# Expert inputs gathered as token rows from DRAM and transposed, in place of one-hot products; twelve weight tiles fetched ahead, not eight

## Chip, cores, metric

The kernel runs on one core of one Trainium2 chip. The metric is the device time of one launch in microseconds (us). TensorE, its weight loads, VectorE, ScalarE, GpSimd and SyncE are called PE, PEld, DVE, ACT, POOL and SP below, as in the profile.

## The reference

Two transformer blocks over 512 tokens of width 1024, in float32. The part that matters here is the mixture of experts at the end of the first block: each token is routed to two of 32 experts, and each expert multiplies its own tokens with its own weights.

```python
g_probs = softmax(hf @ w_group_router + b);  g_gate, g_sel = top_k(g_probs, 1)
e_probs = softmax(e_logits of group g_sel);  e_gate, e_sel = top_k(e_probs, 2)
...
xb = h_pad[tok]                                   # the tokens of one expert
hidden = silu(xb @ w_gate[e]) * (xb @ w_up[e])    # 1024 -> 256
y = (hidden @ w_down[e]) * wt[:, None]            # 256 -> 1024
out = zeros.at[slot_token].add(y)                 # back to the tokens
```

Ahead of it stand differential and latent attention and a cross attention to a memory; behind it the second block: a gated DeltaNet layer, a feed-forward layer, sliding-window attention and another feed-forward layer.

## The kernel before

All activations are kept with the features on the partitions and the 512 tokens along the free axis: `self.x` is eight tiles of 128 by 512. A product of full precision is split in three (`mm3`, L400 to L402): both operands have a high and a low part, and high times high, high times low and low times high are added in PSUM.

The expert stage is `moe` (L1394). It begins with the router: a product with the router weights (`few`), and then a long chain of small DVE operations (L1439 to L1510) from the logits `lt` to `As` (which expert a token goes to), from there by four small products on PE (L1498, L1500) to `posm` (the place of each token among those of its expert, one column for each of the 32 experts). An expert has 64 slots; should one get more tokens, the branch `overflow` does the rest (it isn't taken with these inputs). Beside the router the tokens are turned: 64 PE transposes (L1424) bring the high and the low part of the normalised tokens to two tiles `toks`, with the tokens on the partitions.

The experts are then done in eight rounds `q` of four experts (256 slots), and in a round in two pairs `p`. `gather(q)` makes a matrix `G` of ones and zeros by comparing `posm` with the slot numbers (L1555, DVE), and multiplies `toks` with it on PE (L1565, 64 products of 128 by 256 into `pgt`; ACT copies each bank to `xg`, L1567). That picks the tokens of the slots. Eight small products `pm` (L1571) give for each slot its weight, its token's number and its scale. `gate_up` multiplies with gate and up weights (`pgu`), `down` with the down weights (`py`, both at L1549), and `scatter` (L1615, `psx`) adds the result back to the tokens with another matrix of ones and zeros, `S`.

The expert weights, 192 tiles of 512 KB, come over SP's queue in the order of use (`experts`, `fetch`, L375). `NPRE` of them are fetched during the cross attention, nine more while the keys and values of the second block's memory are made (`mem_kv2`, 192 products of 128 by 256, which stand between router and experts to fill PE), and the rest into a ring of 17 tiles (NPRE plus nine), each as soon as the tile before it there has been read. After `moe` the next stage `gdn` begins by loading its constants `cst_gdn`.

The code isn't executed as written: a scheduler orders the instructions of each engine ahead of time, and each engine then follows its list in order.

Of the kernel before, what the change touches and what calls it, by code (L numbers as in the profile page):

```python
# [19 lines left out]
NPRE=8  # L20
# [258 lines left out]
class K:  # L279
# [1114 lines left out]
    def moe(self):  # L1394
        tc, nc, d = self.tc, self.nc, self.d
        with ExitStack() as st:
            e = lambda **k: st.enter_context(tc.tile_pool(**k))
            mp = e(name="moep", bufs=1)
            I = self.cst("ident")
            self.cst_load(mp, "moe")  # L1400
            rows = mp.tile([P, 36], F32, name="rowsr")
            nc.scalar.dma_start(rows, d["rows2"][:, 24:60].to_broadcast([P, 36]))
            toks = [mp.tile([P, 4, 1024], F32R, name=f"tok{k}") for k in range(2)]
# [4 lines left out]
            gq = e(name="mg", bufs=2)  # L1408

            with ExitStack() as s2:  # L1410
# [8 lines left out]
                for k in range(2):  # L1419
                    for t in range(4):  # L1420
                        for b in range(2):
                            pt = pp.tile([P, 512], F32, name="pl", tag="pl")
                            for c in range(4):
                                nc.tensor.transpose(pt[:, c * P:(c + 1) * P],  # L1424
                                                    hs[4 * b + c][k][:, t * P:(t + 1) * P].bitcast(F32), I)
                            o = toks[k][:, t, b * 512:(b + 1) * 512]
                            if b:
                                nc.vector.tensor_copy(o, pt)
                            else:
                                nc.scalar.activation(o, pt, AF.Copy)  # L1430
# [90 lines left out]

                if self.on("gdn"):
                    self.mem_kv2()

# [8 lines left out]
            r = self.rings["raw"]  # L1533
            used = last // 2 * 2
            self.rings, self.turn = {"raw": r[used:] + [self.pre] * NPRE + r[:used]}, {"raw": 0}
            sw = e(name="ms", bufs=2)
# [13 lines left out]

            def gather(q):

                G = gq.tile([P, 4, 256], F32R, name="G", tag="G")
                for t in range(4):
                    nc.vector.tensor_tensor(G[:, t].rearrange("p (a b) -> p a b", a=4),  # L1555
                                            self.cst("iota64").unsqueeze(1).to_broadcast([P, 4, 64]),
                                            posm[:, t, 4 * q:4 * q + 4].unsqueeze(2).to_broadcast([P, 4, 64]), OP.is_equal)
                xg = xgs[q % 2]
                for c in range(0, 8, 2):
                    pgt = self.pmm.tile([P, 512], F32, name="pgt", tag="mm")  # L1560
                    for j in range(2):
                        cs = slice((c + j) * P, (c + j + 1) * P)
                        for k in range(2):
                            for t in range(4):
                                nc.tensor.matmul(pgt[:, 256 * j:256 * j + 256], toks[k][:, t, cs], G[:, t],  # L1565
                                                 start=k + t == 0, stop=k + t == 4)
                    nc.scalar.activation(xg[:, c:c + 2].rearrange("p a b -> p (a b)"), pgt, AF.Copy)  # L1567
                pm = self.pmm.tile([P, 512], F32, name="pm", tag="mm")
                for a in range(2):
                    for t in range(4):  # L1570
                        nc.tensor.matmul(pm[:, 8 * a:8 * a + 8], G[:, t, P * a:P * a + P], meta[:, t, 2 * q + a],  # L1571
                                         start=t == 0, stop=t == 3)
                ms = gq.tile([P, 2, 8], F32, name="msl", tag="msl")
                nc.vector.tensor_copy(ms, pm[:, 0:16].rearrange("p (a b) -> p a b", a=2))
                nc.vector.tensor_tensor(ms[:, :, 0:2], ms[:, :, 0:2], ms[:, :, 2:4], OP.add)
                nc.vector.tensor_tensor(ms[:, :, 0:2], ms[:, :, 0:2],
                                        self.cst("half").unsqueeze(1).to_broadcast([P, 2, 2]), OP.mult)
                nc.vector.tensor_tensor(ms[:, :, 0:1], ms[:, :, 0:1], ms[:, :, 1:2], OP.add)
                nc.vector.tensor_tensor(ms[:, :, 6:7], ms[:, :, 6:7], ms[:, :, 7:8], OP.add)
                return xg, ms  # L1580
# [37 lines left out]
            xgs = [t.rearrange("p a (b c) -> p (a b) c", b=2).bitcast(F32) for t in self.half()]  # L1618
            g = gather(0)
            sg = gate_up(0, *g)  # L1620
            for q in range(8):
# [556 lines left out]
```

## Time and profile before

| | |
|---|---|
| time, median of 3 runs | 2052.8 us (2051.84 to 2054.6) |
| profiled execution, its time / its span | 2053.69 us / 2051.9 us |
| PE busy | 1984.0 us, 97% of the span |
| DVE, ACT, POOL busy | 50%, 36%, 17% |
| data moved by DMA | 243.44 MB, 119 GB/s over the span |
| expert stage: first expert product, end of the last | 445.72 us, 751.21 us |

The span is what the profile covers; the time lies a little above it. Times in the rows are microseconds from the start of the span, unless marked ns. "Busy" counts the time in which an engine executes instructions; what stands in square brackets behind a row is how long the engine sat idle before it, and what ended that.

### The profile page before, as it was taken

Reading aid. Unit: us, or ns where it says so; the run is one execution under the profiler, and the core shown is the slowest. Engines: PE = TensorE matmul, PEld = TensorE weight load, DVE = VectorE, ACT = ScalarE, POOL = GpSimd, SP = SyncE. Lnnn points to the kernel's source line nnn. Section 1 sums busy time; section 2 is a strip of 40 time slices with the busy share of each in tenths; the row PEclk is TensorE's granted clock in tenths of the full one; section 3 lists DMA queues with packets and bytes.
Section 4 is the critical chain, followed back from the end, with each engine's and each line's share of the span. In section 5 each row is a group of like instructions: output and inputs, shape, how many; then the busy total and the mean of one; then the engine's idle time right before and its main releaser. Section 6 shows DMA issues by size and latency. Waiting matters only on the chain.

```text
span 2051.9 us, 26341 instructions
## 1 busy us (share of the span) xinstructions
PE 1984.0 (97%) x10094; PEld 1521.2 (74%) x10094; DVE 1024.5 (50%) x2067; ACT 735.6 (36%) x1445; POOL 347.7 (17%) x328
## 2 busy tenths in 40 slices
PE   8999999899999999999998999999999999999997
PEld 6768678775555558778877888888876688888886
DVE  7674746632222246788865543343436654434334
ACT  5554644521111133344453332232325642223231
POOL 3012241300000002355411110011111021101111
PEclk9988999999999999999999999999999999999999
DMA  5213114269888852211113222322221033233322
GB/s 191 62 63 108 42 52 159 70 211 391 294 306 331 322 187 64 65 42 53 52 52 102 82 86 85 117 93 81 94 92 42 11 104 102 78 106 105 99 78 70
DMA packets 75458, 243.44 MB, mean 119 GB/s; under 512 B 8825, under 2 KB 11969, under 8 KB 75329
## 3 DMA queue, kind: packets, MB, share of 16 engines
q1 hardware_dynamic: 73520, 240.34, 34.9%
q8 instruction: 81, 1.33, 0.3%
q10 hardware_dynamic: 1664, 1.34, 0.2%
q14 instruction: 49, 0.39, 0.1%
q0 software_dynamic: 144, 0.04, 0.0%
HBM read 235.36 MB, written 6.29 MB: 118 GB/s over the span
## 4 chain that ended last, share of the span: by engine, by line
PE 72%; DVE 3%; DMA 1%; ACT 1%; POOL 1%; issue 0%; DVEq 0%; ACTq 0%
PE mmp L400 16%; PE mmp L401 16%; PE mmp L402 16%; PE pgu L1549 6%; PE psx L1615 3%; PE py L1549 3%; PE pgt L1565 3%; PE sc L1328 1%; DMA raw<-in_w_swa_dram 1%; PE po L749 1%; DVE lo L408 1%; PE tp L962 1%; PE po L1354 1%; PE pt L1340 0%; DVE cv L950 0%; PE sc L729 0%
## 5 line engine op out<-in xcount | busy, mean ns | idle before, releaser
L400 PE MATMUL mmp<-xh,hi 128*128 128x512 f32 (+1 forms) x1328 | 522.2, 393 | 0.8 <-ACT xh L407 0.7
L401 PE MATMUL mmp<-xl,hi 128*128 128x512 f32 (+1 forms) x1328 | 516.9, 389 | 1.0 <-DVE xl L411 1.0
L402 PE MATMUL mmp<-xh,lo 128*128 128x512 f32 (+1 forms) x1328 | 516.7, 389 | 0.0
L407 ACT ACTIVATE hi<-raw 128x1024 fp32r<-128x1024 f32 (+2 forms) x256 | 252.4, 987 | 646.5 <-PE mmp L401 573.7
L408 DVE TENSOR_TENSOR lo<-raw,hi 128x1024 fp32r<-128x1024 f32 (+1 forms) x242 | 280.7, 1161 | 141.5 <-ACT hi L407 138.6
L400 PEld LDWEIGHTS mmp<-xh,hi 128*128 128x128 f32 x1328 | 252.6, 190 | 57.4 <-issue 5.7
L401 PEld LDWEIGHTS mmp<-xl,hi 128*128 128x128 f32 x1328 | 252.6, 190 | 49.9 <-DVE xl L411 1.4
L402 PEld LDWEIGHTS mmp<-xh,lo 128*128 128x128 f32 x1328 | 252.2, 190 | 50.0 <-issue 0.7
L808 POOL TENSOR_TENSOR g<-g,rbc 128x512 f32<-128x512 f32 x44 | 75.1, 1707 | 508.9 <-ACT g L807 508.9
L400 PE MATMUL mmp<-ahi,hi 128*128 128x512 f32 (+1 forms) x374 | 141.9, 380 | 0.0
L401 PE MATMUL mmp<-alo,hi 128*128 128x512 f32 (+1 forms) x374 | 141.9, 380 | 0.0
L402 PE MATMUL mmp<-ahi,lo 128*128 128x512 f32 (+1 forms) x374 | 141.9, 379 | 0.0
L434 POOL TENSOR_TENSOR sqt<-sqt 128x512 f32<-128x512 f32 (+1 forms) x50 | 70.4, 1408 | 252.3 <-ACT sqt L430 236.0
L810 DVE TENSOR_TENSOR a<-mmp,g 128x512 f32<-128x512 f32 x44 | 30.4, 691 | 144.8 <-PE mmp L402 144.8
L806 DVE TENSOR_TENSOR g<-mmp,rbc 128x512 f32<-128x512 f32 x44 | 30.4, 691 | 112.8 <-PE mmp L402 112.7
L400 PEld LDWEIGHTS mmp<-ahi,hi 128*128 128x128 f32 x374 | 70.4, 188 | 14.1
L401 PEld LDWEIGHTS mmp<-alo,hi 128*128 128x128 f32 x374 | 70.4, 188 | 14.0
L402 PEld LDWEIGHTS mmp<-ahi,lo 128*128 128x128 f32 x374 | 70.4, 188 | 14.0
L1565 PEld LDWEIGHTS pgt<-G,tok 128*128 128x128 f32 x512 | 61.6, 188 | 10.9 <-issue 8.9
L1616 DVE TENSOR_TENSOR x<-psx,x 128x512 f32<-128x512 f32 x64 | 43.4, 688 | 47.5 <-PE psx L1615 46.6
L1565 PE MATMUL pgt<-G,tok 128*128 128x256 f32 x512 | 64.6, 282 | 1.0 <-ACT xl L1567 1.0
L1549 PE MATMUL py<-raw,act 128*64 128x512 f32 x256 | 63.9, 599 | 0.2
(519 smaller groups left out, 3001.2 us busy)
## 6 DMA issues: line engine op xcount, KB each, us to landing
raw<-in_w_egu_dram SPq DMA_DIRECT2D x128, 512.0 KB, 7.5
raw<-in_w_gu_dram SPq DMA_DIRECT2D x88, 512.0 KB, 3.5
raw<-in_w_ed_dram SPq DMA_DIRECT2D x64, 512.0 KB, 7.8
raw<-in_w_out_dram SPq DMA_DIRECT2D x24, 512.0 KB, 3.6
raw<-in_w_gdn_dram SPq DMA_DIRECT2D x24, 512.0 KB, 3.6
raw<-in_w_dn_dram SPq DMA_DIRECT2D x32, 384.0 KB, 3.0
raw<-in_w_dn_dram SPq DMA_DIRECT2D x32, 320.0 KB, 2.8
raw<-in_w_qk_dram SPq DMA_DIRECT2D x12, 512.0 KB, 4.3
```

The lines of the kernel that those rows point to most:

```text
L400: mm(ps, a[0], b[0], start=first, stop=False)
L401: mm(ps, a[0], b[1], start=False, stop=False)
L402: mm(ps, a[1], b[0], start=False, stop=last)
L407: nc.scalar.activation(hi, src, AF.Copy)
L408: (eng or nc.vector).tensor_tensor(lo, src, hi.bitcast(F32), OP.subtract)
L434: (nc.vector if i == len(chunks) - 1 else nc.gpsimd).tensor_tensor(acc, acc, s, OP.add)
L806: nc.vector.tensor_tensor(g, pg, bc, OP.mult)
L808: nc.gpsimd.tensor_tensor(g, g, bc, OP.mult)
L1549: nc.tensor.matmul(ps[hb], a[:, hb], w[b][:, o:o + 512], start=first, stop=last)
L1565: nc.tensor.matmul(pgt[:, 256 * j:256 * j + 256], toks[k][:, t, cs], G[:, t], start=k + t == 0, stop=k + t == 4)
L1615: nc.tensor.matmul(psx, ys[k][:, a, c * P:(c + 1) * P], ss[a], start=a + k == 0, stop=a + k == 2)
L1616: nc.vector.tensor_tensor(self.x[c], psx, self.x[c], OP.add)
```

## The change

The token matrix `toks` in SBUF is gone. The tokens (now in one part, in float32: `x` times the gain of the norm, on DVE) are transposed with 32 PE transposes instead of 64 and written to a DRAM tensor `tokd`, one row of 4 KB for each token (eight DMAs, issued by ACT). `gather` is cut in two. `slots(q)` makes `G` and the eight `pm` products as before, forms from them the token number of each slot (`idx`, DVE), and lets POOL issue two indirect DMAs, each of which fetches 128 rows of `tokd` to a tile `rows`. `gather(q, rows)` transposes these rows on PE, 16 transposes in place of 64 products, and ACT copies them to `xg` as before. `slots` is called one round ahead of its `gather`. The scale of the tokens is applied where it was before. The room that `toks` took goes to four `rows` tiles and to four more weight tiles (NPRE 12): the ring has 21 tiles.

```diff
-NPRE=8
+NPRE=12
...
-            toks = [mp.tile([P, 4, 1024], F32R, name=f"tok{k}") for k in range(2)]
+            dp = e(name="tokd", bufs=1, space=bass.MemoryType.DRAM)
+            tokd = dp.tile([T, D], F32, name="tokd")
...
+            def slots(q, room=None):
+                G = gq.tile([P, 4, 256], F32R, name="G", tag="G")
+                for t in range(4):
+                    nc.vector.tensor_tensor(G[:, t].rearrange("p (a b) -> p a b", a=4),
...
+                pm = self.pmm.tile([P, 512], F32, name="pm", tag="mm")
+                for a in range(2):
+                    for t in range(4):
+                        nc.tensor.matmul(pm[:, 8 * a:8 * a + 8], G[:, t, P * a:P * a + P], meta[:, t, 2 * q + a],
+                                         start=t == 0, stop=t == 3)
+                ms = gq.tile([P, 2, 8], F32, name="msl", tag="msl", bufs=3)
+                nc.vector.tensor_copy(ms, pm[:, 0:16].rearrange("p (a b) -> p a b", a=2))
+                idx = gq.tile([P, 2], I32, name="idx", tag="idx", bufs=3)
+                nc.vector.tensor_scalar(idx, ms[:, :, 4], 1.0, 0.0, op0=OP.subtract, op1=OP.max)
+                rows = []
+                for a in range(2):
+                    r = room() if room else gr.tile([P, D], F32, name="rows", tag="rows")
+                    nc.gpsimd.indirect_dma_start(r, None, tokd, bass.IndirectOffsetOnAxis(idx[:, a:a + 1], 0))
+                    rows.append(r)
...
+                return rows, ms
+            def gather(q, rows):
+                xg = xgs[q % 2]
+                for c in range(0, 8, 2):
+                    pgt = self.pmm.tile([P, 2, 2, P], F32, name="pgt", tag="mm")
+                    for j in range(2):
+                        for a in range(2):
+                            nc.tensor.transpose(pgt[:, j, a], rows[a][:, (c + j) * P:(c + j + 1) * P], I)
+                    nc.scalar.activation(xg[:, c:c + 2], pgt.rearrange("p j a b -> p j (a b)"), AF.Copy)
+                return xg
...
-                for k in range(2):
-                    for t in range(4):
-                        for b in range(2):
-                            pt = pp.tile([P, 512], F32, name="pl", tag="pl")
-                            for c in range(4):
-                                nc.tensor.transpose(pt[:, c * P:(c + 1) * P],
-                                                    hs[4 * b + c][k][:, t * P:(t + 1) * P].bitcast(F32), I)
-                            o = toks[k][:, t, b * 512:(b + 1) * 512]
...
+                for b in range(2):
...
+                        nc.vector.tensor_scalar(t, self.x[4 * b + c], self.sm("norm_ffn_g", 4 * b + c, 4 * b + c + 1), None,
+                                                op0=OP.mult)
...
+                            nc.tensor.transpose(pt[:, c * P:(c + 1) * P], xg[c][:, t * P:(t + 1) * P], I)
...
+                        nc.scalar.dma_start(tokd[t * P:(t + 1) * P, b * 512:b * 512 + 512], o)
...
+                sl = slots(0, lambda: r1.tile([P, D], F32, name="rows", tag="xg", bufs=3))
                 if self.on("gdn"):
                     self.mem_kv2()
+                g = gather(0, sl[0]), sl[1]
...
+            gr = e(name="mr", bufs=4)
...
-                for c in range(0, 8, 2):
-                    pgt = self.pmm.tile([P, 512], F32, name="pgt", tag="mm")
-                    for j in range(2):
-                        cs = slice((c + j) * P, (c + j + 1) * P)
-                        for k in range(2):
-                            for t in range(4):
-                                nc.tensor.matmul(pgt[:, 256 * j:256 * j + 256], toks[k][:, t, cs], G[:, t],
-                                                 start=k + t == 0, stop=k + t == 4)
...
-            g = gather(0)
+            sl = slots(1)
...
-                        g = gather(q + 1)
+                        g = gather(q + 1, sl[0]), sl[1]
+                        if q < 6:
+                            sl = slots(q + 2)
```

What the scheduler makes of it is seen at three places. The first is PE between router and experts. Before, the four products that need the router's `As` (L1498, L1500) stand among the products of `mem_kv2` (L400 to L402), 72 of which are ahead of them:

```order
L400 MATMUL mmp_4032<-hi_4028,xh_3899 128x256
L401 MATMUL mmp_4032<-lo_4029,xh_3899 128x256
L402 MATMUL mmp_4032<-hi_4028,xl_3900 128x256
L1498 MATMUL pl_3866<-As_3857,cst_moe_3590 128x128
L1500 MATMUL pl_3866<-As_3857,ones_87 128x96
L1500 MATMUL pl_3866<-As_3857,ones_87 128x64
L1500 MATMUL pl_3866<-As_3857,ones_87 128x32
L400 MATMUL mmp_4058<-hi_4024,xh_3899 128x256
L401 MATMUL mmp_4058<-lo_4025,xh_3899 128x256
L402 MATMUL mmp_4058<-hi_4024,xl_3900 128x256
```

With the change the same four (now L1546, L1548), the transpose for the overflow flag (L1556) and the `pm` products of round 0 (L1421) stand right behind the router's statistics (`stp`, `stb`), and all 192 products of `mem_kv2` follow:

```order
L549 MATMUL mmp<-cst_all,fewo 128x64 x4
L438 MATMUL stp<-ones,sqt 128x1 x4
L451 MATMUL stb<-cst_all,rt 128x128 x4
L1546 MATMUL pl<-As,cst_moe 128x128
L1548 MATMUL pl<-As,ones 128x96
L1548 MATMUL pl<-As,ones 128x64
L1548 MATMUL pl<-As,ones 128x32
L1556 MATMUL pl<-cst_all,mx 1x128
L1421 MATMUL pm<-meta,G 128x8
L438 MATMUL stp<-ones,sqt 128x1 x2
L1421 MATMUL pm<-meta,G 128x8 x7
L451 MATMUL stb<-cst_all,rt 128x128 x2
```

So what the router's DVE chain feeds has moved ahead of the products that stood around it.

The second place is PE in a round of the expert loop. Before, a quarter of `gather` is 16 products (two halves of a bank, each from `tok0` and `tok1`), here the one ahead of four products with down weights:

```order
L1615 MATMUL psx_4913<-S_4673,xh_4669 128x512
L1615 MATMUL psx_4913<-S_4673,xl_4670 128x512
L1565 MATMUL pgt_4990<-G_4985,tok0_3594 128x256 x4
L1565 MATMUL pgt_4990<-G_4985,tok1_3595 128x256 x4
L1565 MATMUL pgt_4990<-G_4985,tok0_3594 128x256 x4
L1565 MATMUL pgt_4990<-G_4985,tok1_3595 128x256 x4
L1549 MATMUL py_5118<-raw_5127,act_5116 64x512
```

With the change the whole of `gather` is 12 transposes, four rows of gate and up products (L1601), and four transposes:

```order
L1636 MATMUL psx<-S,xl 128x512
L1447 MATMUL pgt<-cst_all,rows 128x128 x12
L1601 MATMUL pgu<-raw,xh 64x512 x4
L1447 MATMUL pgt<-cst_all,rows 128x128 x4
L1601 MATMUL pgu<-raw,xh 64x512 x4
L1421 MATMUL pm<-meta,G 128x8 x8
L1601 MATMUL pgu<-raw,xh 64x512 x4
```

The `pm` row there is that of the next round's `slots`, so a round's row numbers are known a whole round ahead of the transposes that use the rows.

The third place is POOL. Before, the last statistics of `mem_kv2` (L419), the branch and the next stage's memset (L944) follow each other there. With the change its list is, with the branch's body left out:

```order
L419 TENSOR_TENSOR rt<-rp,mhalf 128x2
L1431 DMA rows<-tokd,idx 128x1024 x2
L1666 TENSOR_LOAD flag
L1667 COMPARE_AND_BRANCH
...
L1667 UNCONDITIONAL_BRANCH
L1431 DMA rows<-tokd,idx 128x1024 x14
L944 MEMSET pad 128x4 x2
```

The two row transfers of round 0 are issued ahead of the branch, the 14 others in the loop, with nothing else between them.

## Rows read from the trace of the kernel before

**Rows 1.** The profile page: PE's busy time, share and instructions, and the slices of the span (40 of 51.3 us each): PE's busy share in tenths, and what the DMA engines moved.
```profile
PE 1984.0 (97%) x10094; PEld 1521.2 (74%) x10094; DVE 1024.5 (50%) x2067; ACT 735.6 (36%) x1445; POOL 347.7 (17%) x328
PE   8999999899999999999998999999999999999997
GB/s 191 62 63 108 42 52 159 70 211 391 294 306 331 322 187 64 65 42 53 52 52 102 82 86 85 117 93 81 94 92 42 11 104 102 78 106 105 99 78 70
```

**Rows 2.** The chain of work that ended last, in order of time, in the expert stage: start, length, what. From one round's `gather` to that of the next, and the stage's end.
```profile
592.25 5.60 PE pgt L1565 x48
597.85 3.58 PE pgu L1549 x14
601.43 2.07 PE pgt L1565 x16
603.50 0.79 PE pm L1571 x8
604.29 7.88 PE pgu L1549 x34
...
632.89 5.60 PE pgt L1565 x48
...
747.53 3.66 PE py L1549 x16
751.21 4.37 DMA cst_gdn<-in_cst_gdn_dram
```

**Rows 3.** Stretches of the expert stage: stretch, its length, busy time (and instructions) of PE, PEld, DVE, ACT and POOL, PE's granted clock (1.00 is 2.4 GHz), the busy share of the DMA engines, GB/s.
```profile
448.00:513.00 65.00, 64.00 (x317) 31.64 (x314) 13.69 (x26) 9.58 (x17) 0.00 (x0) 0.98 0.98 369
460.00:465.00 5.00, 5.00 (x37) 3.68 (x35) 0.49 (x1) 0.86 (x2) 0.00 (x0) 1.00 1.03 416
500.00:505.00 5.00, 5.00 (x23) 2.47 (x20) 1.08 (x2) 1.39 (x2) 0.00 (x0) 1.00 1.02 407
590.00:610.00 20.00, 20.00 (x124) 12.54 (x122) 4.64 (x13) 3.50 (x5) 0.00 (x0) 1.00 0.71 252
```

**Rows 4.** PE from the router to the first expert product, in order of time: start, length, engine, line, operation, how many, and in brackets the idle time before.
```profile
399.41 1.98 PE L1424 MATMUL pl<-cst_all,xl 128*128 128x128 f32 x16
408.38 0.71 PE L451 MATMUL stb<-cst_all,rt 128*128 128x128 f32 x4 [1.04 <-POOL rt L419]
408.84 0.36 PE L400 MATMUL mmp<-xh,hi 128*128 128x256 f32 x1
409.54 0.42 PE L401 MATMUL mmp<-xl,hi 128*128 128x256 f32 x1
413.06 0.28 PE L401 MATMUL mmp<-xl,hi 128*128 128x256 f32 x1
...
419.05 0.39 PE L1498 MATMUL pl<-As,cst_moe 128*128 128x128 f32 x2
434.43 7.71 PE L1565 MATMUL pgt<-G,tok 128*128 128x256 f32 x64
441.98 0.95 PE L1571 MATMUL pm<-meta,G 128*128 128x8 f32 x8
445.72 2.70 PE L1549 MATMUL pgu<-raw,xh 128*64 128x512 f32 x8 [2.79 <-PEq L1645]
```

**Rows 5.** DVE in the router's chain, in the same form.
```profile
403.34 0.30 DVE L1439 TENSOR_TENSOR lt<-mmp,rt 128x144 f32<-128x144 f32 x1
405.67 0.68 DVE L1428 CAST tok<-pl 128x512 fp32r<-128x512 f32 x1
407.38 0.16 DVE L418 TENSOR_SCALAR rp<-stp 128x2 f32<-128x2 f32 x1
409.24 0.42 DVE L454 COPY rbc<-stb 128x256 f32<-128x256 f32 x1
413.49 0.42 DVE L694 TENSOR_TENSOR mk<-mmp,rbc 128x256 f32<-128x256 f32 x1 [0.94 <-PE mmp L402]
414.53 1.22 DVE L408 TENSOR_TENSOR lo<-raw,hi 128x1024 fp32r<-128x1024 f32 x1
416.09 0.49 DVE L1493 TENSOR_TENSOR As<-oo,g1o 128x32 f32<-128x32 f32 x4
420.07 0.23 DVE L1503 TENSOR_SCALAR As<-As 128x128 f32<-128x128 f32 x1 [1.09 <-PE pl L1500]
420.86 2.76 DVE L1555 TENSOR_TENSOR G<-cst_moe,posm 128x256 fp32r<-128x256 f32 x8
```

**Rows 6.** ACT's first copy of a gathered bank, in the same form.
```profile
436.52 0.60 ACT L1567 ACTIVATE xh<-pgt 128x512 f32<-128x512 f32 x1 [1.36 <-PE pgt L1565]
```

**Rows 7.** DMA issues of the whole program: tensor, queue, how many, KB each, median us from issue to landing.
```profile
raw<-in_w_egu_dram SPq DMA_DIRECT2D x128, 512.0 KB, 7.5
memkv<-kv1d SPq DMA_DIRECT2D x2, 512.0 KB, 10.0
grow<-r POOLq DMA_DIRECT2D x1, 36.0 KB, 2.1
```

More of the change, by code (lines that the diff above doesn't have):

```diff
@@ L1408, in moe @@
             gq = e(name="mg", bufs=2)
+            def slots(q, room=None):
+                G = gq.tile([P, 4, 256], F32R, name="G", tag="G")
+                for t in range(4):
+                    nc.vector.tensor_tensor(G[:, t].rearrange("p (a b) -> p a b", a=4),
+                                            self.cst("iota64").unsqueeze(1).to_broadcast([P, 4, 64]),
+                                            posm[:, t, 4 * q:4 * q + 4].unsqueeze(2).to_broadcast([P, 4, 64]), OP.is_equal)
+                pm = self.pmm.tile([P, 512], F32, name="pm", tag="mm")
[12 more added lines that the diff above has]
+                    rows.append(r)
+                nc.vector.tensor_tensor(ms[:, :, 0:2], ms[:, :, 0:2], ms[:, :, 2:4], OP.add)
+                nc.vector.tensor_tensor(ms[:, :, 0:2], ms[:, :, 0:2],
+                                        self.cst("half").unsqueeze(1).to_broadcast([P, 2, 2]), OP.mult)
+                nc.vector.tensor_tensor(ms[:, :, 0:1], ms[:, :, 0:1], ms[:, :, 1:2], OP.add)
+                nc.vector.tensor_tensor(ms[:, :, 6:7], ms[:, :, 6:7], ms[:, :, 7:8], OP.add)
+                return rows, ms
@@ L1417, in moe @@
                 rt, rbc = self.xstats()
-                for k in range(2):
-                    for t in range(4):
-                        for b in range(2):
-                            pt = pp.tile([P, 512], F32, name="pl", tag="pl")
-                            for c in range(4):
-                                nc.tensor.transpose(pt[:, c * P:(c + 1) * P],
-                                                    hs[4 * b + c][k][:, t * P:(t + 1) * P].bitcast(F32), I)
-                            o = toks[k][:, t, b * 512:(b + 1) * 512]
[L1427 to L1430, printed above, removed]
+                for b in range(2):
+                    xg = []
+                    for c in range(4):
+                        if c % 2 == 0:
+                            two = r1.tile([P, 2, T], F32, name="xg", tag="xg", bufs=3)
+                        t = two[:, c % 2]
+                        nc.vector.tensor_scalar(t, self.x[4 * b + c], self.sm("norm_ffn_g", 4 * b + c, 4 * b + c + 1), None,
+                                                op0=OP.mult)
+                        xg.append(t)
+                    for t in range(4):
+                        pt = pp.tile([P, 512], F32, name="pl", tag="pl")
+                        for c in range(4):
+                            nc.tensor.transpose(pt[:, c * P:(c + 1) * P], xg[c][:, t * P:(t + 1) * P], I)
+                        o = r1.tile([P, T], F32, name="tok", tag="tok", bufs=3)
+                        if t % 2:
+                            nc.vector.tensor_copy(o, pt)
+                        else:
+                            nc.scalar.activation(o, pt, AF.Copy)
+                        nc.scalar.dma_start(tokd[t * P:(t + 1) * P, b * 512:b * 512 + 512], o)
                 V = nc.vector
@@ L1520, in moe @@
                     V.tensor_copy(meta[:, t, :, 6:8], r2[:, :, t].bitcast(F32).unsqueeze(1).to_broadcast([P, 16, 2]))
+                sl = slots(0, lambda: r1.tile([P, D], F32, name="rows", tag="xg", bufs=3))
                 if self.on("gdn"):
                     self.mem_kv2()
+                xgs = [t.rearrange("p a (b c) -> p (a b) c", b=2).bitcast(F32) for t in self.half()]
+                g = gather(0, sl[0]), sl[1]
             self.all_raw(st)
@@ L1616, in scatter @@
                     nc.vector.tensor_tensor(self.x[c], psx, self.x[c], OP.add)
-            xgs = [t.rearrange("p a (b c) -> p (a b) c", b=2).bitcast(F32) for t in self.half()]
-            g = gather(0)
+            sl = slots(1)
             sg = gate_up(0, *g)
```

20 lines of the change are left out of this document (removed).

## The prediction

> **What bounds the kernel now.** The page comes first: PE is busy for 1984.0 of 2051.9 us, and in all slices but a few its digit is 9 [rows 1]. So time is saved only where PE has less to do or waits less, and the question for any change is whether something else then ends last. The slices of the expert stage (445 to 751 us) are the ones in which DMA is busiest: 391 GB/s in the first full slice, then 294 to 331 [rows 1]. The chain in order of time tells which of the two ends last there: from 592.25 to 632.89 us it consists of PE work without a break, 40.6 us for a round, of which `gather` is 5.60 + 2.07 = 7.67 us and `pm` 0.79 us [rows 2]. The stretches say the same from the other side: at 590 to 610 us PE is busy for 20.00 of 20 us while the DMA engines stand at 0.71 and 252 GB/s, whereas they reached 407 to 416 GB/s at 460 and 500 us [rows 3]. PE bounds the loop and the weights follow; but a round moves 24 tiles of 512 KB, 12.6 MB in 40.6 us or 310 GB/s, so the second limit isn't far below.
>
> **The loop.** Seven of the eight `gather`s lie in the loop; each loses 7.67 us and gets 16 transposes. A run of 16 transposes of the same shape took 1.98 us, the last one's tail of about 0.3 us included [rows 4], so 0.11 us each and 1.8 us for 16. Something comes on top that the old form hid: a bank of PSUM is filled by four transposes in 0.45 us, but ACT takes 0.60 us to copy it [rows 6], and there are two banks. Where twelve transposes stand in a row, the third group waits until the first bank is copied, some 0.55 us by these lengths. In sum 7 x (7.67 - 1.8 - 0.55) = 37 us less. The stage from its first expert product to the end of the last, 445.72 to 751.21 or 305.5 us [rows 2, 4], becomes 268.5 us if PE remains the limit.
>
> **The way to the loop.** Here the order of the lists matters. Before, PE went from the second `stb` (408.38 us) straight to the products of `mem_kv2` at 408.84, and the router's DVE chain ran beside them; the product that needs `As` came at 419.05 [rows 4]. Now that product, the `pm` products of round 0 and that `stb` stand ahead of all 192. PE follows its list, so it idles until the chain is through. How long: the chain begins with `lt` at 403.34 and `As` ends at 416.58 [rows 5]. I leave its start where it is. In that time DVE also did a `tok` cast (0.68), an `rbc` copy (0.42), an `mk` with its wait (0.94 + 0.42) and a `lo` (1.22) [rows 5], which now come elsewhere: 3.7 us off, `As` at about 412.9. From the product at 419.05 to the end of `G` at 423.62 [rows 4, 5] it was 4.6 us, so `G` ends at 417.7 with a little for the hand-over. Behind it come the flag's maximum (about 0.3 us) and the second statistics, which from `rp` at 407.38 to the first product at 408.84 took 1.5 us [rows 4, 5]. The 192 products start at 419.5, 10.7 us later than before. They took 25.6 us with a slow start: 0.42 us at 409.54 against 0.28 at 413.06 [rows 4], which is the lower of the two clock levels after PE's waits. The wait is now longer, so the slow start remains; the end is at 445.1. Then `gather(0)` with its `pm` took 434.43 to 442.93, 8.5 us [rows 4]. With 16 transposes in a row, each pair of banks waiting for its copies, it is about 2.6 us, and 0.9 for `pm`: 448.6. The branch keeps its 2.79 us [rows 4]. The first expert product comes at 451.4 instead of 445.72: 5.7 us lost, though two pieces of work became shorter.
>
> **What costs nothing, and its cover.** The 32 transposes saved at the router (3.6 us of PE) are put at nothing, because PE waits for the chain there anyway. The eight products `x` times gain on DVE are at most of the `tok` cast's length (0.68 us [rows 5]), and four casts go: between 0 and 2.7 us on the chain's start, taken as 0. The first two row transfers run under the 25.6 us of `mem_kv2`, the others have a round between issue and use. No row shows such a transfer; the nearest are POOL's only DMA with data (36 KB, 2.1 us), a weight tile of the same 512 KB (7.5 us) and a 512 KB load behind many others (10.0 us) [rows 7]. A pair is so between 4 and 20 us; I take 15, near the weight tiles since the size and the crowding are theirs, and it is covered either way. The twelve tiles instead of eight save nothing by themselves, because the chain shows no weight wait in a round [rows 2]; they are a reserve of four tiles for the next point.
>
> **The transfers.** 192 weight tiles and 16 row tiles of 512 KB must come. When the loop starts, 21 and 2 are there; 185 or 97.0 MB remain. They can start when the first tile has been read, 2.70 us behind the first product [rows 4], at 454.1. At 407 GB/s, the saturated stretch, they take 238 us, and end at 692; at 369 GB/s, the mean over 65 us with its dips [rows 3], 263 us, and end at 717. The last four products of a pair then need 3.7 us [rows 2]: between 696 and 721. PE by itself ends at 451.4 + 268.5 = 719.9. The two limits nearly meet, and since a full ring makes the queue pause whenever PE does other work, I add 5 us for late weights: 725.
>
> The Trainium skill (DMA: Bandwidth & Descriptors, "Where 436 GB/s comes from") puts what one core gets from HBM at about 358 GB/s. By that the transfers would take 271 us, end the stage at 728.8 and leave 2030 us. The trace doesn't agree: 391 GB/s over a whole slice and 416 over 5 us [rows 1, 3], so the measurement decides.
>
> **Sum.** 751.2 - 725 = 26.2 us less (37 in the loop, 5.7 lost ahead of it, 5 for the weights). What follows, the wait of 4.37 us for `cst_gdn` [rows 2] and the later stages, stays. The profiled execution took 2053.69 us with a span of 2051.9, 0.9 above the median of 2052.8; the same difference from the median gives 2027 us.
>
> **The rivals.** First, the transfers become the limit. For it: 26 tiles in a round of 35 us are 13.6 MB or 389 GB/s, which no stretch of 65 us held. Against: the reserve of 21 tiles. At 345 GB/s, between the mean of 369 and the 331 at which the gain is gone (97.0 MB in 751.2 - 454.1 - 3.7 = 293 us), they take 281 us, the stage ends at 739, gain 12, time 2040.
>
> Second, the wait ahead of `mem_kv2` is much shorter. For it: less PE and ACT work stands ahead of `lt`. Against: the lengths of the chain, all from rows, and a list that PE follows: it sat idle for 1.04 us ahead of `stb` although the products behind it could start at once [rows 4]. Without the wait the loop starts 10.7 us earlier and the gain is 37: 2016.
>
> Third, slower: the rows come late, each round, and PE stands at its first transpose. The point at which it decides: a pair has one round of 35 us, and the 26 us are used up if each of seven rounds waits 3.7 us more, so if one transfer of 128 rows takes over 19 us. With 25 us each it would be 7 x (50 - 35) = 105 us of waits, 79 more than now: 2132. The 2.1 and 10.0 us [rows 7] speak against it, POOL's empty list too; that no gather by index is in the trace leaves it a chance.
>
> **Chances and range.** The forecast 0.57 (2018 to 2036: 5 us of late weights or none, the chain's start up to 2.7 us later, half of the gap to either neighbour), the transfers 0.24 (0.19 still faster, 0.02 no change, 0.03 slower), the shorter wait 0.13, the late rows 0.06. That is faster by over 0.2% (4.1 us, about what a measurement here can tell) 0.89, the same 0.02, slower 0.09. The range is 2010 to 2046: down to the shorter wait without late weights, up into the transfers' case.
>
> **What would show it.** Right: in the router's part one PE wait of over 10 us for DVE's `As`, with the products behind it at the lower clock at first; the first `pgu` near 451; rounds of 35 us with `pgt` of about 2 us; DMA at 0.95 or more through the stage and a few waits of `pgu` and `py` for weights; no wait of `pgt` for `rows`. Wrong: rounds of over 37 us with PE waiting for `raw`, which is the first rival; the first `pgu` at 441, the second; `pgt` waiting for `rows`, the third. The forecast is also wrong if the stages after 760 us change, which I take as untouched.

## The result, and the profile after

The change made the kernel slower: 2063.3 us median (2058.7 to 2064.2) against 2052.3 us of the kernel before on the same chip, a ratio of 1.0053 with a 95% interval of 1.0042 to 1.0063. The forecast was 2027 us. The profiled execution after has a span of 2061.1 us, 9.2 more than before.

The page of the changed kernel, in the form of [rows 1]:

```profile
span 2061.1 us, 25591 instructions
PE 1968.6 (96%) x9678; PEld 1468.0 (71%) x9678; DVE 1027.9 (50%) x2079; ACT 732.8 (36%) x1441; POOL 360.1 (17%) x344
PE   8999999789999989999999999999999999999997
GB/s 190 62 67 103 42 55 196 110 184 404 393 368 334 302 152 75 62 41 52 52 57 91 87 90 85 113 93 82 101 93 41 11 103 102 78 100 110 97 80 69
```

PE is busy 15.4 us less, 416 instructions fewer, and yet the end comes later. PE's digits are lower in the 8th and 9th slice (7 and 8, before 8 and 9), which lie at 361 to 464 us, mostly ahead of the expert stage, and in the 15th (8, before 9), around its end. PE from the router to the first expert product, and the last rows of the stage from the chain, answer to [rows 4] and to the end of [rows 2]:

```profile
412.01 0.80 PE L1546 MATMUL pl<-As,cst_moe 128*128 128x128 f32 x2 [8.41 <-DVE As L1541]
419.49 0.56 PE L400 MATMUL mmp<-xh,hi 128*128 128x256 f32 x1
444.70 0.60 PE L1447 MATMUL pgt<-cst_all,rows 128*128 128x128 f32 x4
447.33 1.05 PE L1421 MATMUL pm<-meta,G 128*128 128x8 f32 x8
454.79 1.97 PE L1601 MATMUL pgu<-raw,xh 128*64 128x512 f32 x4 [6.40 <-PEq L1667]
...
759.62 1.89 PE py L1601 x8
761.53 4.60 DMA cst_gdn<-in_cst_gdn_dram
```

So the stage starts at 454.79 instead of 445.72 (9.1 us later) and ends at 761.5 instead of 751.2. From first product to end it lasts 306.7 us; before, 305.5. From there to the last `stp` of the program it is 1291.4 us after and 1292.6 before. The loss is as large as the later start (the stage 1.2 us longer and what follows 1.2 shorter), and the 37 us that the loop was to give are missing entirely.

Weights aren't where they went. PE's waits in the stage (455 to 762 us), all but the branch's 6.4 us ahead of its first product: who waited for whom, us in total, times, longest:

```profile
PE pgt L1447 <- ACT xl L1448: 3.0, 3, 1.6
PE psx L1636 <- ACT xh L410: 2.0, 3, 1.2
PE pgt L1447 <- DVE x L1637: 1.4, 3, 0.7
PE psx L1636 <- DVE x L1637: 1.2, 2, 0.6
PE pgu L1601 <- DMA raw<-in_w_egu_dram: 0.8, 2, 0.6
PE py L1601 <- DVE xl L411: 0.6, 1, 0.6
PE pgt L1447 <- ACT xh L1448: 0.4, 1, 0.4
```

That is 9.4 us (before: 1.0, all of it `pgt` for ACT's copy `xl`), of them 0.8 for weights. PE is busy, then, but with what? PE within a round, in order of time (`pgu` and `py` are 64 columns wide, `psx` 128; each 64-wide product leaves two records, 768 for the stage's 384 products, so x8 are four products):

```profile
608.70 1.07 PE L1601 MATMUL pgu<-raw,xh 128*64 128x512 f32 x2
609.70 0.73 PE L1636 MATMUL psx<-S,xl 128*128 128x512 f32 x2
610.36 1.93 PE L1601 MATMUL pgu<-raw,xh 128*64 128x512 f32 x6
612.23 0.50 PE L1636 MATMUL psx<-S,xh 128*128 128x512 f32 x1
...
634.68 1.94 PE L1601 MATMUL pgu<-raw,xl 128*64 128x512 f32 x8
636.54 1.06 PE L1421 MATMUL pm<-meta,G 128*128 128x8 f32 x8
```

From the start of a `pgu` group to the start of what follows: two records 1.00 us, six 1.87, eight 1.86. `both` gives each weight tile pair one product for columns 0 to 63 and one for 64 to 127; the two run side by side and take 0.86 us together. Six records are three products, one of them without its partner in this group, and they take as long as four. The group of one product costs more than half as much as that of four. And PE's list now has many such groups. One late round of it, from a `gather` to the next, in products, before and after:

```
before: pgt48 pgu7 pgt16 pm8 pgu17 psx8 pgu8 ph2 psx8 py8 ph2 psx12 py8 psx4
after:  pgt12 pgu4 pgt4 pgu4 pm8 pgu8 psx1 py1 psx3 py7 ph2 pgu5 psx2 pgu3 psx2 pgu4
        psx4 pgu1 psx4 pgu3 psx4 py1 psx4 py3 ph2 py1 psx4 py3 psx4
```

Before, the 64-wide products of the stage stand in 44 unbroken runs, after in 86.

### The profile page after: what moved, and what is told of

Read it like the earlier page. It is cut to its first block, busy times and chain, and to the rows that moved or that the text cites. A ratio compares the mean times of both kernels' runs of the same rounds, so it can differ in the third digit from the quotient of the medians.

```text
span 2061.1 us, 25591 instructions
## 1 busy us (share of the span) xinstructions
PE 1968.6 (96%) x9678; PEld 1468.0 (71%) x9678; DVE 1027.9 (50%) x2079; ACT 732.8 (36%) x1441; POOL 360.1 (17%) x344
## 4 chain that ended last, share of the span: by engine, by line
PE 70%; DVE 4%; DMA 2%; ACT 1%; POOL 1%; issue 0%; DVEq 0%; ACTq 0%
PE mmp L400 16%; PE mmp L401 16%; PE mmp L402 16%; PE pgu L1601 6%; PE psx L1636 3%; PE py L1601 3%; PE sc L1328 1%; DMA raw<-in_w_swa_dram 1%; PE po L749 1%; DVE lo L408 1%; PE tp L962 1%; PE pgt L1447 1%; PE po L1354 1%; DMA raw<-in_w_egu_dram 0%; PE pt L1340 0%; DVE cv L950 0%
## 5 line engine op out<-in xcount | busy, mean ns | idle before, releaser
L400 PE MATMUL mmp<-xh,hi 128*128 128x512 f32 (+1 forms) x1328 | 522.5, 394 | 1.4 <-ACT xh L407 0.7
L402 PE MATMUL mmp<-xh,lo 128*128 128x512 f32 (+1 forms) x1328 | 516.4, 389 | 0.0
L400 PEld LDWEIGHTS mmp<-xh,hi 128*128 128x128 f32 x1328 | 252.7, 190 | 58.0 <-issue 5.7
L402 PEld LDWEIGHTS mmp<-xh,lo 128*128 128x128 f32 x1328 | 252.4, 190 | 50.0 <-issue 0.7
L400 PE MATMUL mmp<-ahi,hi 128*128 128x512 f32 (+1 forms) x374 | 141.9, 380 | 0.0
L402 PE MATMUL mmp<-ahi,lo 128*128 128x512 f32 (+1 forms) x374 | 141.9, 379 | 0.0
L810 DVE TENSOR_TENSOR a<-mmp,g 128x512 f32<-128x512 f32 x44 | 30.4, 691 | 144.7 <-PE mmp L402 144.7
L806 DVE TENSOR_TENSOR g<-mmp,rbc 128x512 f32<-128x512 f32 x44 | 30.4, 691 | 112.5 <-PE mmp L402 112.5
L400 PEld LDWEIGHTS mmp<-ahi,hi 128*128 128x128 f32 x374 | 70.4, 188 | 14.1
L402 PEld LDWEIGHTS mmp<-ahi,lo 128*128 128x128 f32 x374 | 70.4, 188 | 14.0
L1601 PE MATMUL pgu<-raw,xh 128*64 128x512 f32 x256 | 71.9, 618 | 6.4 <-PEq L1667 6.4
L1601 PE MATMUL py<-raw,act 128*64 128x512 f32 x256 | 74.9, 616 | 0.6 <-DVE xl L411 0.6
L1601 PE MATMUL pgu<-raw,xl 128*64 128x512 f32 x256 | 70.6, 604 | 0.8 <-DMA raw<-in_w_egu_dram 0.8
## 6 DMA issues: line engine op xcount, KB each, us to landing
raw<-in_w_egu_dram SPq DMA_DIRECT2D x128, 512.0 KB, 10.1
```

The lines of the kernel that those rows point to most:

```text
L400: mm(ps, a[0], b[0], start=first, stop=False)
L402: mm(ps, a[1], b[0], start=False, stop=last)
L806: nc.vector.tensor_tensor(g, pg, bc, OP.mult)
L810: nc.vector.tensor_tensor(a, pu, g, OP.mult)
L1601: nc.tensor.matmul(ps[hb], a[:, hb], w[b][:, o:o + 512], start=first, stop=last)
```

## The experiments

Theory A: the list of PE is what changed; products without a partner and changes between 64-wide and 128-wide work ate the gain. Theory B: the first rival of the prediction, the transfers set the stage's length. Prices for A from the rows above: 0.857 us for a pair or a lone product, 0.235 for a `psx`, 0.11 for a transpose, 0.15 for each change of width (eight records alone 1.86 us against 1.71).

**1. Partners tied together** (changed kernel). The half whose tile lands last goes first, the other is tied behind it:

```
-                for b in range(2):
+                one = None
+                for b in (1, 0):
                     hb = slice(64 * b, 64 * b + 64)
-                    nc.tensor.matmul(ps[hb], a[:, hb], w[b][:, o:o + 512], start=first, stop=last)
+                    with tc.issue_after(one) if one else ExitStack():
+                        one = nc.tensor.matmul(ps[hb], a[:, hb], w[b][:, o:o + 512], start=first, stop=last).ins
```

> The changed kernel, with the two products of each `both` kept next to each other in PE's list (the second half of the tile pair first, the first half tied behind it). In the changed kernel 34 of the 192 product pairs of a tile pair are pulled apart in that list by other products, in the kernel before 13; here 3. The runs of half-wide products between full-wide ones fall from 86 to 59. Theory A (broken pairs): a product that stands without its partner takes as long as the pair, 0.86 us, and each change between half-wide and full-wide products costs 0.15 us. By these prices PE's list of the expert stage sums to 296.6 us in the changed kernel and to 261.5 here, so 35 us less: 2028 us if the weights keep up, 2040 if half of the gain turns into waits for weights. Theory B (the weight transfers set the stage's length, the pulled-apart list is only what waiting for weights looks like): the time stays within 5 us of 2063.

Measured: 2042.5 us, ratio to the kernel before 0.9955 (0.9939 to 0.9971). The same transfers, the same work, and the stage is 278.8 us long instead of 306.7. The two stages, the changed kernel first, in the form of [rows 3]:

```profile
454.90:761.50 306.60, 297.32 (x1188) 114.73 (x1188) 81.98 (x157) 48.03 (x78) 13.26 (x14) 0.99 0.85 323
453.30:732.10 278.80, 265.60 (x1187) 111.73 (x1187) 81.51 (x157) 47.70 (x78) 13.24 (x14) 0.99 0.93 355
```

PE is busy 31.7 us less with as many records, and the same bytes come faster. Theory B is out as the cause. The total fell by less than the stage's 27.9 us, because PE's order in the later stages changed with the list too, and PE waits there at other places: from the stage's end to the last `stp` it now takes 1305.8 us instead of 1291.4 (in a profiled execution that itself lies 5.4 us above the median). That is why stages are compared below, and totals only beside them.

**2. The same in the kernel before.**

> The kernel before with the same tie of the two products of each `both`; 8 broken pairs instead of 13, 42 runs of half-wide products instead of 44. Theory A: the list sums to 300.2 instead of 305.1 us, so 4.9 us less, 2047 us. Theory B says nothing of broken pairs: 2052 us.

Measured: 2050.2 us, ratio 0.999 (0.9979 to 1.0000); the stage 302.8 instead of 305.4 us. The direction of A, half its size, and at the edge of what can be told from no change.

**3. Eight tiles ahead** (changed kernel, `NPRE=8`).

> The changed kernel with eight weight tiles fetched ahead instead of twelve (that part of the change undone). Its list has 42 broken pairs instead of 34 and sums to 303.8 instead of 296.6 us. Theory A: 7 us more, 2070 us, and not much beyond it, as the waits for weights were 1 us in the changed kernel. Theory B: the smaller reserve makes the waits for weights longer by four tiles at the rate of 409 GB/s, 5 us or more in several rounds, 2075 to 2090 us. If the fetching of twelve is itself what did the harm: 2045 to 2055.

Measured: 2071.1 us, ratio 1.0093 (1.0074 to 1.0113), the stage 314.5 us. As A says, and PE's waits in the stage name no weights at all: the largest entry is 8.4 us of `psx` for ACT's `xh`. So it isn't the reserve as such. By the table below the list is 5.4 us longer and PE's waits 5.1; that the waits too come from the order isn't shown.

**4. Partners moved apart by one place** (kernel before). In each tile pair the order is half 1, 1, 0, 0, in the next one 0, 0, 1, 1:

```
-                for b in range(2):
+                for b in ((1, 0), (0, 1))[turn]:
                     hb = slice(64 * b, 64 * b + 64)
-                    nc.tensor.matmul(ps[hb], a[:, hb], w[b][:, o:o + 512], start=first, stop=last)
+                    for ps, a, o, first, last in parts:
+                        with tc.issue_after(one) if one else ExitStack():
+                            one = nc.tensor.matmul(ps[hb], a[:, hb], w[b][:, o:o + 512], start=first, stop=last).ins
```

> The price by itself: the kernel before, with the four products of each tile pair in the order half 1, half 1, half 0, half 0, and the next tile pair in the order 0, 0, 1, 1, so that in each four only the two in the middle are partners side by side. The work, the tiles and the changes between half-wide and full-wide products (39 runs, before 44) stay. Theory A: three times 0.86 us instead of two for each of 96 tile pairs, 82 us more, less some 11 us for the 13 pairs that were broken anyway: 2115 to 2135 us. If neighbours in the list don't matter: 2052 us within 5.

Measured: 2053.8 us, ratio 1.0013 (1.0004 to 1.0023). A in this form fell. Eight down products in the new order:

```profile
622.71 3.72 PE L1552 MATMUL py<-raw,act 128*64 128x512 f32 x16
626.36 0.44 PE L1601 MATMUL ph<-cst_all,sg 128*128 128x128 f32 x2
```

3.65 us from start to start, four times 0.857 and a little: a partner needn't be the neighbour, it is enough that it stands in the same run. The Trainium skill (TensorE: Matmul & The Clock Gate, "The mechanism") has matmuls start and end strictly in the order of the list. By that these eight would have taken six times 0.857, or 5.1 us, so the row doesn't agree. Theory A was therefore put anew: a run of 64-wide products between 128-wide ones takes 0.857 us for each product of its longer half. Counted so, the stage has 203 units before, 219 after, 193 in experiment 1, 198 in 2, 225 in 3 and 206 here, where 192 is the least.

**5. PE's list written by hand** (changed kernel). All products of the loop are tied one behind the other: down products of a pair and gate and up products of the next in one run, then `ph`, half a scatter and the transposes or `pm`:

```
+            def pe(f, *a, **k):
+                with tc.issue_after(at[0]) if at[0] else ExitStack():
+                    at[0] = f(*a, **k).ins
...
+                    def fill():
+                        piece = lambda c: scatter(*old, [4 * a + c]) if old else None
+                        if a == 0 and q < 7:
+                            new.append((gather(q + 1, sl[0], pe, piece), sl[1]))
+                            return
+                        for c in range(4):
+                            piece(c)
...
+                            if q < 6:
+                                new.append(slots(q + 2, pe=pe))
+                    py = down(p, cur, fill)
```

> The changed kernel with PE's list of the expert stage written out by hand: per expert pair one unbroken run of half-wide products (the down products of one pair, the gate and up products of the next), then one stretch of full-wide work (`ph`, half of the scatter of the round before, and the 16 transposes or the `pm` products). 17 runs of half-wide products instead of 86, none without its partner. Theory A (broken pairs and changes of width): the list sums to 246.0 us, in the changed kernel 296.6 and in the run with tied pairs 261.5; with the 9 us of PE waits as they are, 50 us less: 2013 us. Theory B (transfers): at the 409 GB/s of the saturated stretch, the 97 MB that are left at the first product last 237 us, so PE must wait for weights: 2022 to 2035 us, with DMA at 0.97 or more until about 700 us. If the list has nothing to do with it: 2063.

Measured: 2027.3 us, ratio 0.9886 (0.987 to 0.9903), the stage 276.7 us. It lies in B's range, but its waits say otherwise:

```profile
PE pgt L1600 <- DMA rows<-tokd,idx: 10.6, 6, 2.1
PE psx L1600 <- DVE x L1647: 7.7, 17, 1.3
```

None is for weights. The hand-written list asks for a round's rows only one pair ahead (the changed kernel: a whole round), and two transfers of some 9 us each, one issued 1.2 us behind the other, aren't there in time. The waits cost more than their own length. Behind three of the six PE's granted clock stood at 0.50, the lower of its two levels (1.2 GHz), for 3.4 us each; one of the waits, and the stretch from 534 us in the form of [rows 3]:

```profile
532.55 0.55 PE L1600 MATMUL pgt<-cst_all,rows 128*128 128x128 f32 x3 [1.82 <-DMA rows<-tokd,idx]
534.00:537.40 3.40, 3.37 (x13) 2.42 (x11) 1.16 (x2) 0.60 (x1) 0.00 (x0) 0.50 1.02 408
```

**6. The same list in the kernel before.**

> The kernel before (one-hot products, eight tiles ahead) with the same hand-written list: 17 runs, no product without its partner. Theory A: the list sums to 286.9 instead of 305.1 us, 18 us less: 2034 us. Against the changed kernel with this list it isolates what the change itself does when the list is the same: 40.9 us less PE work in the stage, the later start of the stage (about 9 us) against it, so the changed kernel with the list should be 32 us faster than this one if the transfers keep up, and 10 to 20 us if they don't.

Measured: 2038.3 us, ratio 0.9937 (0.992 to 0.9953), the stage 292.2 us. With like lists the change takes 15.5 us off the stage in spite of the row waits. The times differ by 11.0 us, where 32 was expected with transfers that keep up; the late transfers are those of the rows, not of the weights.

**7. The wait ahead of the loop** (5, and `mem_kv2` ahead of the router's chain):

```
+                if self.on("gdn"):
+                    self.mem_kv2()
+                    done = self.last_mm
+                with tc.high_priority(offset=2000):
                     V = nc.vector
...
+                with tc.issue_after(done):
+                    g = gather(0, sl[0]), sl[1]
```

> The changed kernel with the hand-written list and, in addition, the code of `mem_kv2` ahead of the router's chain, which has the higher priority: the product of `As` now stands behind 38 of the 192 products of `mem_kv2`, the `pm` products of round 0 behind some 70, the transposes of round 0 behind all of them. If the later start of the stage is the wait of PE for `As`, the first `pgu` comes 8 to 10 us earlier than in the run with the list alone, near 444 us, and the time falls by as much as long as PE sets the pace; if the transfers do, by less, since they too can start only with the first product. If it is something else, no change.

Measured: 2019.8 us, ratio 0.985 (0.9833 to 0.9866). PE no longer waits for `As`, and the first `pgu` comes 7.4 us earlier than in experiment 5:

```profile
414.38 0.39 PE L1552 MATMUL pl<-As,cst_moe 128*128 128x128 f32 x2
434.72 2.78 PE L1447 MATMUL pgt<-cst_all,rows 128*128 128x128 f32 x16
445.76 1.98 PE L1605 MATMUL pgu<-raw,xh 128*64 128x512 f32 x4 [7.15 <-PEq L1696]
```

The time fell by 7.5 us, as it must if PE sets the pace. By itself this doesn't part the theories, since the weight transfers too can start only with the first product; experiments 9 and 10 do. The wait at the branch did not shrink.

**8. The price of lone products by itself** (6, the last two products of one half of each `gate_up` behind the 128-wide stretch):

```
-                        both(ps, xg[:, k, sl], w, 512 * c, k == 0, k == 7)
+                        both(ps, xg[:, k, sl], w, 512 * c, k == 0, k == 7, (1, 0) if u < 3 or p == 0 else (p % 2,))
+                def rest():
+                    for c in range(2 if p else 0):
+                        both(ps, xg[:, 6 + c, sl], w, 512 * c, False, c == 1, (1 - p % 2,))
+                    return act_up(p, ps, ms)
```

> The price of a product without its partner by itself: the kernel before with the hand-written list, in which the last two products of one half of each gate-and-up group are moved behind the stretch of full-wide work, in turns for the one and the other half. Work, tiles and the 17 runs stay; the longer half of each run has two products more. Counted by the longer half of a run: 222 instead of 192 units of 0.857 us, so 25.7 us more than the kernel before with the list alone. If a product without its partner costs no more than half of a pair: the same time as that kernel.

Measured: 2068.7 us, 30.4 more than experiment 6; the stage 313.5 us, 21.3 more (the two profiled executions differ by 23.6 us). The 64-wide products by themselves, from the start of each record to that of the next, take 24.3 us more (169.6 and 193.9), near the 25.7 expected; PE's waits are 2.4 less. One run in experiment 6, from its first row to `ph`:

```profile
598.59 3.65 PE L1546 MATMUL py<-raw,act 128*64 128x512 f32 x16
602.07 7.04 PE L1546 MATMUL pgu<-raw,xh 128*64 128x512 f32 x32
609.04 0.44 PE L1546 MATMUL ph<-cst_all,sg 128*128 128x128 f32 x2
```

and one with the same 24 products here:

```profile
605.74 1.50 PE L1546 MATMUL pgu<-raw,xh 128*64 128x512 f32 x3
...
610.57 7.40 PE L1546 MATMUL pgu<-raw,xh 128*64 128x512 f32 x27
617.90 0.44 PE L1546 MATMUL ph<-cst_all,sg 128*128 128x128 f32 x2
```

10.45 us for 12 + 12, 12.16 us for 14 + 10 (the rows between are left out): 1.71 more, twice 0.857. Theory A in its second form stands.

**9. Rows asked for early** (7, with `slots` behind the transposes of the round before, as in the changed kernel):

```
                             new.append((gather(q + 1, sl[0], pe, piece), sl[1]))
+                            if q < 6:
+                                new.append(slots(q + 2, pe=pe))
                             return
...
-                            if q < 6:
-                                new.append(slots(q + 2, pe=pe))
```

> The run with list and front, with the `pm` products and the row transfers of a round asked for one expert pair earlier, directly behind the transposes of the round before, as the changed kernel has them. In the run before it PE waited 10.8 us at its transposes for `rows`, six times about 2 us, since a pair of rows lands only about 10 us after it is asked for. Theory A (PE's own list and its waits set the pace): these waits go, 8 to 11 us less, 2009 to 2012 us. Theory B (the transfers, at 409 GB/s from 460 to 640 us, set the pace): the wait moves from the rows to the weights, 2017 to 2020 us.

Measured: 2006.7 us, ratio 0.9792 (0.9769 to 0.9816): 44 us less than the kernel before beside it (2050.9), 57 less than the changed one. The stage is 258.0 us, shorter than the 268.5 of the prediction, and 34.2 us shorter than experiment 6 with one-hot products and the same kind of list: the 37 us of the prediction, nearly. PE's wait for `rows` is gone from its table, whose largest entry, but for the branch, is now

```profile
PE psx L1605 <- DVE x L1652: 6.8, 19, 0.6
```

Stretches, in the form of [rows 3]:

```profile
460.00:500.00 40.00, 38.00 (x194) 17.40 (x192) 10.72 (x29) 9.58 (x17) 3.82 (x4) 1.00 1.03 410
540.00:580.00 40.00, 38.96 (x186) 19.11 (x186) 15.67 (x31) 6.85 (x12) 1.88 (x2) 1.00 1.03 408
620.00:660.00 40.00, 38.27 (x187) 18.91 (x184) 12.40 (x23) 8.70 (x15) 1.88 (x2) 1.00 1.03 409
```

PE at 38 to 39 of 40 us and DMA full, side by side.

**10. No row transfers in the loop** (9, six gathers not done).

> The same with the row transfers of rounds 2 to 7 left out: their transposes read the rows of round 1 once more (so part of the computation is changed, six of the eight gathers are not done). 12 transfers of 512 KB or 6.3 MB less, 15 us of the transfers at 409 GB/s. Theory A (PE): the same time as the run with the rows asked for early, within 3 us. Theory B (transfers): up to 15 us less than it.

Measured: 2017.4 us, ratio 0.9833 (0.9812 to 0.9854), yet the stage is 259.1 us, as in experiment 9. So the transfers don't set the pace even there, though they come near: DMA falls to some 380 GB/s from 580 us on, and nothing is gained.

```profile
620.00:660.00 40.00, 38.61 (x189) 18.89 (x186) 11.79 (x23) 8.13 (x14) 0.00 (x0) 1.00 0.99 380
```

The 11 us of difference in the total lie behind the stage (to the last `stp` 1303.5 against 1292.2 us), where the order of work has changed again.

The stages together. Units are products of the longer halves; the list is units x 0.857, the 128-wide work, and 0.15 for each change of width. Each stage is read from one execution, and executions of one kernel lie up to 9 us apart, so differences of 2 or 3 us tell nothing. The kernel before, timed again beside the experiments, took 2050.6 us (1 to 4), 2051.1 (5 to 8) and 2050.9 (9 and 10):

| kernel | runs | units | list us | PE waits us | stage us | time us |
|---|---|---|---|---|---|---|
| before | 44 | 203 | 303.5 | 1.0 | 305.4 | 2052.3 |
| after | 86 | 219 | 290.8 | 9.4 | 306.6 | 2063.3 |
| 1 tied | 59 | 193 | 259.9 | 13.1 | 278.8 | 2042.5 |
| 2 before, tied | 42 | 198 | 298.6 | 2.5 | 302.8 | 2050.2 |
| 3 eight ahead | 87 | 225 | 296.2 | 14.5 | 314.5 | 2071.1 |
| 4 apart | 39 | 206 | 304.6 | 1.0 | 307.9 | 2053.8 |
| 5 list | 17 | 192 | 246.0 | 18.6 | 276.7 | 2027.3 |
| 6 before, list | 17 | 192 | 286.9 | 3.0 | 292.2 | 2038.3 |
| 7 front | 17 | 192 | 246.0 | 19.1 | 274.4 | 2019.8 |
| 8 lone | 17 | 222 | 312.6 | 0.6 | 313.5 | 2068.7 |
| 9 rows early | 17 | 192 | 246.0 | 7.8 | 258.0 | 2006.7 |

List and waits together fall short of the measured stage by 0.3 to 6.4 us in nine of the eleven, and by 9 to 12 us in experiments 5 and 7. Much of that is the clock: counting half of each stretch of the stage at a granted clock of 0.50 as lost, experiment 5 lost 8.0 us and experiment 7 lost 4.9, the other nine none to 3.9. Some 4 us remain open in each of the two.

## Why the prediction was wrong, point by point

**The loop: the step that failed.** The prediction took PE's list of the loop as it was and only exchanged the gather, 37 us less. The exchange itself came as costed: summed from the start of each record to that of the next, `pgt` took 54.7 us of the stage before and 18.8 after, waits included, 35.9 less. But the 64-wide products took 25.2 us more (182.6 and 207.8), `psx` 9.5 more (57.3 and 66.8) and the rest some 2.5 more, which is all of the gain. By the list's prices, the 128-wide work went from 116.5 to 77.4 us, 39.1 less (with 8 scatter products more in the stage); 16 more units cost 13.7 us, 84 more changes of width 12.6, PE's waits 8.4, together 34.7. Of the other 5.6 the lower clock accounts for 1.8. The order that did this was in the document, at the second of its three places: `pgt` x12, `pgu` x4, `pgt` x4, `pgu` x4, `pm` x8, `pgu` x4. It was read for what had moved and not for what it breaks apart, and [rows 2] has prices of long runs only, though even there 14 `pgu` records (7 products) took 3.58 us and 16 `py` records (8 products) 3.66. What makes the list so is argued, not shown: where work of fixed length left PE, the program that writes the order found gaps while it waited for weights, and filled them.

**The way to the loop: right but for one term.** The chain's `As` ended at 411.96 (predicted 412.9), the 192 products began at 419.49 (419.5), the transposes at 444.70 (445.1), `pm` ended at 448.4 (448.6). That it fits to a tenth at 419.49 is luck in part: `lt` began at 401.51, 1.8 us before the time that was left as it was, and the chain to `As` took 10.5 us where 9.6 was summed, the way from the product behind it to the end of `G` 5.5 us instead of 4.6. The wait of PE was 8.4 us where "over 10" was the mark; the products behind it began at the lower clock, as said (0.50 from 419.5 to 423 us). Only the branch was off: 6.40 us instead of the 2.79 of [rows 4], so 454.79 and not 451.4. Kernels with rows by index have 6.3 to 7.5 us there, those with one-hot products 2.8 to 3.5; the trace names PE's own sequencer, and what lengthens it stays open. That the wait for `As` is a matter of order, the second rival's condition, experiment 7 shows.

**What costs nothing.** The rows were covered: no transpose waited for them in the changed kernel. A transfer, issue to landing in the whole program (after, in the form of [rows 7]):

```profile
rows<-tokd,idx POOLq DMA_INDIRECT x16, 9.2
```

so a pair takes some 10 us where 15 were assumed. Experiment 5 shows the third rival's mechanism, at the size of 2 us a round, as soon as the cover is one pair instead of one round. The twelve tiles were put at nothing; with eight it is 7.8 us slower, without a wait of PE for weights (experiment 3).

**The transfers: right as far as tested.** 5 us of late weights were assumed, 0.8 came, though the changed kernel's PE was too slow to put it to the test. Experiment 9 does: it holds 408 to 410 GB/s from 460 to 660 us, the 407 of [rows 3] over a stretch forty times as long. "DMA at 0.95 or more through the stage" was wrong, with 0.85 in the mean: PE was too slow to ask for more. The limit of about 358 GB/s from HBM for one core, which the prediction had from the Trainium skill (DMA: Bandwidth & Descriptors, "Where 436 GB/s comes from") and set aside, doesn't hold for this core, by the same rows.

**The rivals.** Rounds of over 37 us were the sign of the first rival. They came (306.7 / 8 = 38.3 us) without its cause, PE waiting for `raw`. The list had no chance of its own among the rivals, and the range of 2010 to 2046 had no term for it. The rivals that could end slower, late rows above all, named other mechanisms.

## What to carry to other kernels

Where a change removes work from a scheduled loop, count the new list before summing durations: how many runs of each tile width there are, and how many products in them lack a partner. Tie products that run side by side together in the code, so that a schedule can't part them, and check the length of the stage itself, as the order of everything behind it changes too, here by up to 14 us. A transfer that was covered by a round is covered only as long as the list asks for it a round ahead.

## What the runs showed of the hardware

- A run of 64-wide products (512 columns each, float32) costs 0.86 us for each product of its longer column half, wherever in the run the partners stand (8 products in 3.65 us in the order 1 1 0 0 0 0 1 1; 24 in 10.45 us when balanced, 12.16 us at 14 to 10).
- Each change between 64-wide and 128-wide products costs about 0.15 us: PE's weight load idles 0.81 us ahead of a 128-wide load behind a 64-wide product and 0.29 us within a run (after, weight loads):

```profile
622.47 0.19 PEld L1636 LDWEIGHTS psx<-S,xh 128*128 128x128 f32 x1 [0.81 <-issue]
626.22 0.14 PEld L1601 LDWEIGHTS py<-raw,act 128*64 128x64 f32 x1 [0.29 <-issue]
```

- A transfer of 128 rows of 4 KB by index takes POOL 0.94 us to issue and lands after 9.2 us in a stage whose weight tiles take 10.1 (both medians, after).
- One core alone drew 408 to 410 GB/s for 200 us (experiment 9).
- Behind waits of about 2 us PE's granted clock fell to 0.50 three times in experiment 5, for 3.4 us each; a `psx` took 0.42 us there and 0.235 at 1.00.
